# Moving 640 columns of each tile from ScalarE to VectorE in a batch-norm kernel that streams through three buffers

## The chip, the cores and the metric

The kernel runs on 1 core of one Trainium2 chip. The metric is the device time of one execution in microseconds (us), as the median of several runs. Experiments of one batch ran on the same chip as new runs of the kernel before, and each is compared with those.

## The reference

```python
# x: (32, 256, 128, 128) float32; the four parameters: 256 channels each
return gamma * (x - mean) / np.sqrt(var + eps) + beta
```

Per channel this is one multiplication and one addition, `x * scale + shift`. The kernel must read 537 MB and write 537 MB; there is next to no arithmetic per byte.

## The kernel before

The input is seen as 64 tiles of 128 partitions x 16384 columns (8 MB each; 64 KB in a row). The program keeps three tiles in on-chip memory; tile `i` uses buffer `i % 3`. Three streams run side by side: SyncE issues loads, VectorE and ScalarE compute in place, ScalarE issues stores. The parts that matter:

```python
NBUF = 3
STEP = 2560       # VectorE's first piece of a tile
VCOLS = 14336     # VectorE takes columns 0..VCOLS, ScalarE the rest
VLAST = 9216      # the same for the last tile
...
for i in range(1, NT):                                  # SyncE: the loads
    if turn:
        nc.sync.wait_ge(stored[s], 16 * turn)           # buffer free: store i-3 has landed
    inst = nc.sync.dma_start(out=bufs[s][:], in_=xr[i]).then_inc(loaded[s], 16)
    if turn:
        inst._wait_ge(vdone, 2 * (i - 1) + 1)           # tile i-1 landed, its first piece done
...
for i in range(1, NT):                                  # VectorE
    vector_part(i, 0, STEP)._wait_ge(*landed(i))
    vector_part(i, STEP, VLAST if i == last else VCOLS)
for i in range(last):                                   # ScalarE
    nc.scalar.wait_ge(vdone, 2 * (i + 1))               # VectorE is done with tile i
    inst = scalar_part(i, VCOLS)
    if i:
        inst._wait_ge(stored[(i - 1) % NBUF], ...)      # hold until store i-1 has landed
    store(i)                                            # after its own piece (adone)
```

Two waits in it are no data dependencies. A load waits for VectorE's first piece of the tile before it, and ScalarE's piece waits for the store before it. The time in which the load queue has nothing to do, from the landing of one load to the first packet of the next, is called the load gap below; the same on the other queue is the store gap. ScalarE's piece lies in the store gap, VectorE's first piece in the load gap.

## Time and profile before

| | kernel before |
|---|---|
| median of the first 3 runs | 2484.97 us (2483.55 to 2486.38) |
| VectorE busy, ScalarE busy | 508.8 us, 139.8 us |
| mean DMA rate over the span | 432 GB/s |
| ScalarE's piece; VectorE's first piece | 2.09 us; 1.61 us |
| from tile to tile (mean of 50) | 38.69 us |

Two more: from the list of DMA issues on the page, a store's median time from issue to landing,

```profile
out_dram<-t ACTq DMA_DIRECT2D x64, 36.5
```

and, from SyncE's own waits (line, what it waited for, us in total, times, longest), what holds back a load:

```profile
SPq L101 <- DMA out_dram<-t: 1398.1, 61, 68.8
SPq L102 <- DVE t L130: 985.0, 61, 16.2
```

The waits come in program order, first for the freed buffer, then for VectorE's first piece of the tile before. The second still takes some 16 us each time, so the buffer is free long before the load goes, and the loads pace themselves.

### The profile page before, as it was taken

The page shows a single profiled execution, that of the slowest core. Times are in us where ns is not written, and L with a number is a line of the kernel's source. Part 1 is how long each engine was busy: PE and PEld are TensorE (multiplying, and loading weights), DVE is VectorE, ACT ScalarE, POOL GpSimd, SP SyncE. Part 2 cuts the span into 40 slices and gives each one's busy share as a digit, 9 for nine tenths or more (in the row PEclk, how much of TensorE's full clock was granted, in tenths as well). Part 3 has the DMA queues.
Part 4 walks back from the last instruction along what each step waited for, and adds up shares of the span by engine and source line. Part 5 has one row for each costly group of instructions (what it writes and reads, how often), then busy time and mean ns, then how long its engine had stood idle before and what let it go on. Part 6 is the DMA issues. An engine that isn't in the chain of part 4 may idle for free.

```text
span 2483.3 us, 516 instructions
## 1 busy us (share of the span) xinstructions
DVE 508.8 (20%) x139; ACT 139.8 (6%) x66; POOL 0.2 (0%) x4
## 2 busy tenths in 40 slices
DVE  3122121221212212122121221212212122121220
ACT  0000000000000000000000000000000000000001
POOL 0000000000000000000000000000000000000000
DMA  9999999999999999999999999999999999999999
GB/s 415 430 439 434 428 436 436 435 433 430 432 433 438 430 432 433 435 424 437 437 428 436 438 436 429 437 435 430 436 437 436 430 437 435 429 437 435 433 433 408
DMA packets 18708, 1073.85 MB, mean 432 GB/s; under 512 B 2128, under 2 KB 2192, under 8 KB 2192
## 3 DMA queue, kind: packets, MB, share of 16 engines
q1 hardware_dynamic: 9488, 536.94, 50.1%
q10 hardware_dynamic: 9216, 536.88, 49.9%
q14 instruction: 4, 0.03, 0.0%
HBM read 536.94 MB, written 536.87 MB: 432 GB/s over the span
## 4 chain that ended last, share of the span: by engine, by line
DMA 93%; DVE 4%; another core or an unknown queue 1%; ACT 0%; issue 0%; SPq 0%; DVEq 0%
DMA t<-in_x_dram 93%; DVE t L130 4%; ACT t L141 0%; SPq L91 0%; DVE rows L89 0%; SPq L95 0%; DVE eps_t L107 0%; DVEq L198 0%; SPq L70 0%
## 5 line engine op out<-in xcount | busy, mean ns | idle before, releaser
L130 DVE TENSOR_SCALAR t<-t,scale_t,shift_t 128x11776 f32<-128x11776 f32 (+2 forms) x128 | 505.3, 3989 | 1930.4 <-DMA t<-in_x_dram 1930.2
L141 ACT ACTIVATE t<-t,shift_t,scale_t 128x2048 f32<-128x2048 f32 x64 | 138.2, 2159 | 2299.3 <-DMA out_dram<-t 2276.6
L108 DVE STREAM_TRANSPOSE turned<-rows 32x1024 f32<-32x1024 f32 x1 | 1.2, 1233 | 12.5 <-DMA rows<-in_running_mean_dram 12.5
L115 ACT ACT_TABLE_LOAD x1 | 1.3, 1283 | 0.9 <-SPq L70 0.9
L89 DVE MEMSET rows<- 32x1024 f32 x1 | 0.9, 912 | 1.2 <-SPq L70 1.2
L115 ACT ACTIVATE std_t<-par,eps_t 128x2 f32<-128x2 f32 x1 | 0.3, 296 | 14.7 <-DVE par L113 14.7
L113 DVE COPY par<-turned 32x8 f32<-32x8 f32 x4 | 0.6, 161 | 0.1
L122 DVE RECIPROCAL rstd_t<-std_t 128x2 f32<-128x2 f32 x1 | 0.2, 166 | 0.4 <-ACT std_t L115 0.4
L125 DVE TENSOR_TENSOR shift_t<-par,ms_t 128x2 f32<-128x2 f32 x1 | 0.2, 161 | 0.0
L124 DVE TENSOR_TENSOR ms_t<-par,scale_t 128x2 f32<-128x2 f32 x1 | 0.2, 161 | 0.0
L123 DVE TENSOR_TENSOR scale_t<-par,rstd_t 128x2 f32<-128x2 f32 x1 | 0.2, 160 | 0.0
L187 POOL MEMSET const-bfloat16-1.0<- 128x1 bf16 x1 | 0.1, 101 | 0.0
L187 POOL MEMSET const-uint8-127<- 128x1 uint8 x1 | 0.1, 101 | 0.0
L187 POOL MEMSET const-float32-0.0<- 128x1 f32 x1 | 0.1, 98 | 0.2 <-issue 0.2
L187 POOL MEMSET const-float32-1.0<- 128x1 f32 x1 | 0.1, 98 | 0.0
L107 DVE MEMSET eps_t<- 128x1 f32 x1 | 0.1, 59 | 0.1
## 6 DMA issues: line engine op xcount, KB each, us to landing
t<-in_x_dram SPq DMA_DIRECT2D x2, 4096.0 KB, 16.5
out_dram<-t ACTq DMA_DIRECT2D x64, 36.5
t<-in_x_dram SPq DMA_DIRECT2D x63, 37.0
rows<-in_running_var_dram SPq DMA_DIRECT2D x1, 16.0 KB, 11.3
rows<-in_gamma_dram SPq DMA_DIRECT2D x1, 16.0 KB, 11.1
rows<-in_beta_dram SPq DMA_DIRECT2D x1, 16.0 KB, 10.9
rows<-in_running_mean_dram SPq DMA_DIRECT2D x1, 16.0 KB, 11.3
```

The lines of the kernel that those rows point to most:

```text
L89: zeroed = step(nc.vector.memset(rows[:], 0.0))
L107: step(nc.vector.memset(eps_t[:], eps))
L108: step(nc.vector.transpose(out=turned[:], in_=rows[:]), fetched, 16 * NPAR)
L113: placed = step(nc.vector.tensor_copy(out=flat[q * B : (q + 1) * B], in_=blocks[:, :, q, 0]))
L115: nc.scalar.activation(out=std_t[:], in_=var_t, func=mybir.ActivationFunctionType.Sqrt, bias=eps_t[:], scale=1.0,)._wait_ge(vec, placed).t ...
L122: step(nc.vector.reciprocal(out=rstd_t[:], in_=std_t[:]), act, 1)
L123: step(nc.vector.tensor_mul(out=scale_t[:], in0=gamma_t, in1=rstd_t[:]))
L124: step(nc.vector.tensor_mul(out=ms_t[:], in0=mean_t, in1=scale_t[:]))
L125: ready = step(nc.vector.tensor_sub(out=shift_t[:], in0=beta_t, in1=ms_t[:]))
L130: return nc.vector.tensor_scalar(out=t[:, first:end], in0=t[:, first:end], scalar1=scale_t[:, cb : cb + 1], scalar2=shift_t[:, cb : cb + 1 ...
L141: return nc.scalar.activation(out=t[:, first:], in_=t[:, first:], func=mybir.ActivationFunctionType.Identity, bias=shift_t[:, cb : cb + 1] ...
L187: nc = _bacc.Bacc("TRN2", target_bir_lowering=False, num_devices=1)
```

## The change

The intent is to shorten what stands between the landing of one store and the issue of the next: ScalarE gets 1408 columns in place of 2048, VectorE the 640 others, for which it has time.

```diff
-VCOLS = 14336
+VCOLS = 14976
```

## The prediction

> **What bounds the kernel now.** I read first the page's totals (busy engines, the 40 slices, the DMA queues), because they say which resource is full:
>
> ```profile
> DVE 508.8 (20%) x139; ACT 139.8 (6%) x66; POOL 0.2 (0%) x4
> ...
> DMA  9999999999999999999999999999999999999999
> ...
> DMA packets 18708, 1073.85 MB, mean 432 GB/s; under 512 B 2128, under 2 KB 2192, under 8 KB 2192
> ...
> q1 hardware_dynamic: 9488, 536.94, 50.1%
> q10 hardware_dynamic: 9216, 536.88, 49.9%
> ```
>
> VectorE works a fifth of the time and ScalarE a sixteenth. The 16 DMA engines are busy in every slice, and the loads (q1) and stores (q10) take half of the engines' time each: 50.1% + 49.9% = 100%.
>
> Second I read the groups of instructions with shapes kept apart, and the waits, because there ScalarE seems to be in the way:
>
> ```profile
> L130 DVE TENSOR_SCALAR t<-t,scale_t,shift_t 128x11776 f32<-128x11776 f32 x62 | 397.3, 6408 | 0.0
> L141 ACT ACTIVATE t<-t,shift_t,scale_t 128x2048 f32<-128x2048 f32 x63 | 131.8, 2093 | 2286.9 <-DMA out_dram<-t 2276.6 <-DVE t L130 10.2
> L130 DVE TENSOR_SCALAR t<-t,scale_t,shift_t 128x2560 f32<-128x2560 f32 x63 | 101.6, 1613 | 1929.0 <-DMA t<-in_x_dram 1929.0
> L141 ACT ACTIVATE t<-t,shift_t,scale_t 128x7168 f32<-128x7168 f32 x1 | 6.4, 6360 | 12.5 <-DMA t<-in_x_dram 12.5
> ```
>
> By the program, ScalarE holds back its piece of a tile until the store of the tile before has landed, computes 2.09 us, and only then issues the next store. So in every tile the store queue has nothing to do for the landing, those 2.09 us and the start of the next DMA. That looks like a serial 2.09 us per tile, and it is what the change cuts.
>
> Third I asked whether the engines really idle in that gap. The timeline of two tiles gives the times, and the table of stretches the DMA load; its columns after the stretch are its length, the busy time and count of VectorE, ScalarE and GpSimd, the clock, the DMA share and GB/s:
>
> ```profile
> 1041.67 2.09 ACT L141 ACTIVATE t<-t,shift_t,scale_t 128x2048 f32<-128x2048 f32 x1 [36.53 <-DMA out_dram<-t]
> 1043.80 0.34 ACTq L154 DMA_DIRECT2D out_dram<-t  x1
> 1056.18 7.94 DVE L130 TENSOR_SCALAR t<-t,scale_t,shift_t 128x2560 f32<-128x2560 f32 x2 [30.69 <-DMA t<-in_x_dram]
> 1080.80 2.09 ACT L141 ACTIVATE t<-t,shift_t,scale_t 128x2048 f32<-128x2048 f32 x1 [37.03 <-DMA out_dram<-t]
> ```
>
> ```profile
> 100.00:500.00 400.00, 79.36 (x20) 21.64 (x11) 0.00 (x0) 1.00 1.00 434
> ...
> 1042.00:1047.00 5.00, 0.00 (x0) 1.76 (x1) 0.00 (x0) 1.00 1.03 446
> 1056.20:1061.40 5.20, 5.20 (x2) 0.00 (x0) 0.00 (x0) 1.00 1.02 441
> ```
>
> The second row is a store gap: ScalarE computes, and the DMA share is still 1.03 (rounding of packets that cross the edge). The DMA view of the same 5 us says who fills it: the load queue alone, with 102.9% of the engines' time and 34 packets, none of the store queue. The third row is the mirror image, a load gap (a landed tile waits for VectorE's first 1.61 us before the next load is issued), and there the store queue alone fills the engines. In the packet records of the trace a 64 KB packet takes 2.418 us on its engine, in either gap as in between, and from 1.95 us after the start to 2481.7 us no moment has fewer than 16 packets in flight. **The kernel is bound by the bytes through the 16 DMA engines.** The chain of waits names one line above all, and it goes through loads and VectorE's first piece, with ScalarE at 0%:
>
> ```profile
> DMA t<-in_x_dram 93%; DVE t L130 4%; ACT t L141 0%; SPq L91 0%; DVE rows L89 0%; SPq L95 0%; DVE eps_t L107 0%; DVEq L198 0%; SPq L70 0%
> ```
>
> **What the Trainium skill says.** "DMA: Bandwidth & Descriptors", section "Queues, rings and completion order" (its paragraph on arbitration): each engine goes round-robin between the queues that have work, a packet at a time. The trace agrees: away from the gaps, packets of q1 and q10 alternate on an engine, and in a gap the other queue's packets follow each other without a pause. The same page, "Where 436 GB/s comes from", gives a ceiling of 435 GB/s for the 16 engines; the trace has 434 in the steady stretches, so nothing is left there. "ScalarE: Activation LUTs", section "What ACT_TABLE_LOAD costs", gives 0.833 ns per element of a row whatever the function; the two ACTIVATE rows above give (6360 - 2093) / (7168 - 2048) = 0.833, the same.
>
> **The change, part by part.** No instruction is added or removed; the order of instructions on each engine is the same, only the shapes differ. 63 of the 64 tiles change; the last keeps its split at 9216.
> - ScalarE: 640 columns fewer in each of 63 tiles, 640 x 0.833 = 533 ns. An ACTIVATE goes from 2.09 to 1.56 us, and 63 x 0.533 = 33.6 us of work leave ScalarE (139.8 to about 106).
> - VectorE: 640 columns more. The slope from its two rows is (6408 - 1613) / (11776 - 2560) = 0.520 ns per column, so +333 ns a tile: the large piece goes from 6.41 to 6.74 us, 63 x 0.333 = 21.0 us more in all (508.8 to about 530).
> - VectorE's first piece (2560 columns, 1.61 us), which lets the next load go, does not change, so the load gap does not.
> - On the path to a store: ScalarE waits for VectorE too. The tile that lands at 1056.18 is done by VectorE at 1064.12, and ScalarE takes it at 1080.80, since it must wait for the store ahead: 16.7 us of slack, of which the extra 0.33 us takes 2%. The store is therefore issued 0.53 us sooner after the store ahead has landed: its gap (landing at about 1041.67 to the issue at 1043.80) shrinks from 2.13 to 1.60 us.
> - What that saves of the span: the engines were full of load packets in that gap. Of the 0.53 us nothing is saved; the store takes turns a little sooner and the load, which had them, gets them a little later. Steady state: 0 us.
> - Head: the first store comes after VectorE's second piece of tile 0 (+0.33 us) and ScalarE's (-0.53 us), 0.2 us sooner; loads fill the engines then. Tail: the last tile's split is unchanged and it waits for bytes. Together I put 0 to 0.3 us on both.
>
> The sum is 0 to -0.3 us. As a check from above: all 1073.85 MB at the steady 434 GB/s take 2474 us, so even an ideal head and tail would give only 11 us (0.4%).
>
> **Rivals.**
> 1. The store chain sets the time. Then the whole 33.6 us would come off: 2451 us, 1.4% less. For it speaks ScalarE's wait of 2276.6 us for stores, which looks like a serial loop of 38.6 us a tile. Against it: the DMA share of 1.03 in the gap. A store lands in 36.5 us because it shares the engines with loads; it has no speed of its own to which a gap is added. Even this rival stays within 2%.
> 2. VectorE becomes the bound, or the store starts to wait for it: +21 us at most, 2506 us (0.8% slower). Against it: 20% busy, 16.7 us of slack per tile.
> 3. The phases of the two streams shift. Now a store lands 14.5 us before a load does, and each gap is covered by the other queue. A shorter store gap (unchanged load gap) favours the stores in the round-robin; they could run ahead, until a store waits for its own tile and both gaps fall together, and then engines could idle. How far: the store's first packet reaches the engines 3.1 to 3.4 us after its issue; 0.53 us is 22% of a 2.418 us packet, so per tile on about a fifth of the engines the store would get in a turn sooner, and these are engines whose load part ends early anyhow (the packet records show six that end their load some 3 to 4 us ahead of the last), so neither landing need move. Should the stores gain on the loads all the same, they have the 16.7 us of slack to use up first, and then VectorE's wait stops them while the next load has already been issued. I expect at most a few us here, 1% for more than 50 us.
> 4. Contention or bad luck of a run: single tiles now and then take 1 us longer (37.7 in place of 36.5 us of waiting), and the three times before spread from 2483.55 to 2486.38.
>
> **Range and chances.** From 2484.97 us I take 0.2 for the head and leave the rest: **2484.8 us**. The range is the spread of runs of the kernel before widened by about 2 us on each side for a shifted phase: 2481.5 to 2488.5. Faster by over 2% would need 2435 us, less than the bytes take at 434 GB/s, so 0.5%; slower by over 2% (2535 us) needs 0.8 us of idle engines in every tile: 1%; within 2%: 98.5%.
>
> **What would show it.** In the profile after: ScalarE's row at about 1.56 us with about 106 us in all, VectorE's large piece at 6.74 us, the DMA share still 1.00 and 433 to 434 GB/s in the steady stretches, a time from tile to tile still near 38.65 us, and the waits of ScalarE for stores grown by what its work lost (2276.6 + 33.6 = about 2310 us). Step by step wrong would be: a period of 38.1 us (rival 1), ScalarE waiting for VectorE in steady state (2 or the end of 3), a DMA share under 0.99 or a store that lands much nearer to the load (3). The prediction fails if the engines turn out to have idle time between the two queues that the records hide, or if a changed phase opens such time.

## The result, and the profile after

| | before | after |
|---|---|---|
| median of 6 runs each | 2482.99 us (2482.05 to 2486.38) | 2483.53 us (2482.64 to 2487.21) |
| ratio | | 1.0003, 95% interval 0.9990 to 1.0016 |
| ScalarE busy, VectorE busy | 139.8, 508.8 us | 106.2, 529.9 us |
| from tile to tile (mean of 50 in the profiled run) | 38.69 us | 38.73 us |

A ratio is the mean time of one kernel's runs over that of the other's of the same rounds, so it is not quite the ratio of the medians. Nothing came of the change: same, within 0.16%. (The profiled run of the changed kernel was the slowest of its six, 2487.21 us.)

The page's totals after:

```profile
DVE 529.9 (21%) x139; ACT 106.2 (4%) x66; POOL 0.2 (0%) x4
...
DMA  9999999999999999999999999999999999999999
...
q1 hardware_dynamic: 9488, 536.94, 50.1%
q10 hardware_dynamic: 9216, 536.88, 49.8%
```

The groups with shapes kept apart (busy us and mean ns of one; after the second bar the idle time before them and its causes):

```profile
L130 DVE TENSOR_SCALAR t<-t,scale_t,shift_t 128x12416 f32<-128x12416 f32 x62 | 418.0, 6742 | 0.0
...
L141 ACT ACTIVATE t<-t,shift_t,scale_t 128x1408 f32<-128x1408 f32 x63 | 98.2, 1559 | 2322.6 <-DMA out_dram<-t 2311.7 <-DVE t L130 10.9
```

The two pieces changed exactly as their slopes say, and ScalarE's wait for stores grew from 2276.6 to 2311.7 us: the 35 us look like the 33.6 us of work that went away. The list of DMA issues says the same per tile, since a store now lands later after its issue:

```profile
out_dram<-t ACTq DMA_DIRECT2D x64, 37.1
```

The timeline shows the distances inside a tile:

```profile
1041.60 1.56 ACT L141 ACTIVATE t<-t,shift_t,scale_t 128x1408 f32<-128x1408 f32 x1 [37.03 <-DMA out_dram<-t]
1043.18 0.34 ACTq L154 DMA_DIRECT2D out_dram<-t  x1
1056.14 8.27 DVE L130 TENSOR_SCALAR t<-t,scale_t,shift_t 128x2560 f32<-128x2560 f32 x2 [30.37 <-DMA t<-in_x_dram]
1080.27 1.56 ACT L141 ACTIVATE t<-t,shift_t,scale_t 128x1408 f32<-128x1408 f32 x1 [37.12 <-DMA out_dram<-t]
```

From the landing of a store (ScalarE's start) to its issue it is now 1.58 us, before 2.13 us. But the load lands 14.54 us after ScalarE's start, where before it was 14.51, and the next ScalarE start follows at 38.67 us. The store was offered 0.5 us earlier and finished no earlier. The table of stretches shows the steady state and a store gap (columns: length, busy time and count of VectorE, ScalarE and GpSimd, clock, DMA share, GB/s):

```profile
100.00:500.00 400.00, 82.70 (x20) 16.49 (x11) 0.00 (x0) 1.00 1.00 435
1042.00:1046.50 4.50, 0.00 (x0) 1.15 (x1) 0.00 (x0) 1.00 1.08 466
```

The engines are as full as they were. A short stretch like the second gives a share a little off 1, as packets that start in it are counted whole.

### The profile page after: what moved, and what is told of

It reads as the page before. It is cut to its first block, busy times and chain, and to the rows that moved or that the text cites. A ratio compares the mean times of both kernels' runs of the same rounds, so it can differ in the third digit from the quotient of the medians.

```text
span 2485.4 us, 516 instructions
## 1 busy us (share of the span) xinstructions
DVE 529.9 (21%) x139; ACT 106.2 (4%) x66; POOL 0.2 (0%) x4
## 4 chain that ended last, share of the span: by engine, by line
DMA 92%; DVE 5%; another core or an unknown queue 2%; ACT 0%; issue 0%; SPq 0%; DVEq 0%
DMA t<-in_x_dram 92%; DVE t L130 4%; ACT t L141 0%; SPq L91 0%; DVE rows L89 0%; DVE eps_t L107 0%; DVEq L198 0%; SPq L70 0%
## 5 line engine op out<-in xcount | busy, mean ns | idle before, releaser
L130 DVE TENSOR_SCALAR t<-t,scale_t,shift_t 128x12416 f32<-128x12416 f32 (+2 forms) x128 | 526.4, 4154 | 1911.9 <-DMA t<-in_x_dram 1911.8
L141 ACT ACTIVATE t<-t,shift_t,scale_t 128x1408 f32<-128x1408 f32 x64 | 104.6, 1634 | 2335.6 <-DMA out_dram<-t 2311.7
```

Of the source, the lines that this page charges most:

```text
L130: return nc.vector.tensor_scalar(out=t[:, first:end], in0=t[:, first:end], scalar1=scale_t[:, cb : cb + 1], scalar2=shift_t[:, cb : cb + 1 ...
L141: return nc.scalar.activation(out=t[:, first:], in_=t[:, first:], func=mybir.ActivationFunctionType.Identity, bias=shift_t[:, cb : cb + 1] ...
```

## The experiments

The theory of the prediction is that the gap on one queue costs nothing because the other queue fills the engines. Its rivals are a store chain that does set the time (with the gain lost elsewhere), and a phase between the two streams that the gap helps to set. If the gap is simply free, it is free at any size; so the first batch made much larger changes to the same waits.

To see the order of packets, the packet records of the trace were strung together. The records don't name the engine; a record was put behind the one that ended as it started, so single swaps between engines are possible. Below, L is a 64 KB packet of a load and S of a store, `S.` and `L.` are a store's and a load's closing 4-byte packet alone, a number in brackets the duration in ns where it was over 2500 (2418 otherwise), and `--1.51--` an idle engine for 1.51 us. One engine's row from the kernel before:

```
S L S L S. L L L S L S L. S S S L S L S L S L S. L
```

The store ends (`S.`), load packets run alone until the next store comes, both take turns, the load ends (`L.`), store packets run alone, and so on: eight packets of each in a tile (the closing ones not counted), 16 x 2.418 = 38.69 us, which is the measured time from tile to tile.

### Shorter still: ScalarE 128 columns (e1_scalar128)

```diff
-VCOLS = 14336
+VCOLS = 16256
```

> ScalarE computes 128 columns ahead of each store (about 0.49 us by the slope of 0.833 ns a column), VectorE the rest: three times the step of the change, in the same direction. Theory 'the DMA engines are full, so the store gap is free': 2483 us, the same as before. Rival 'the store chain sets the time': 63 x 1.60 us = 101 us less, 2383 us. Rival 'phase': the store gap is now shorter than the load gap by over a us, the stores gain on the loads until a store waits for its own tile; both gaps then fall near each other and engines idle: slower than 2535 us, and ScalarE is seen waiting for VectorE.

Measured: **2562.86 us** (2558.87 to 2569.82), ratio 1.0332, 95% interval 1.0315 to 1.0350. Taking three times as much from ScalarE's piece made the kernel 3.3% slower. Both "free at any size" and "the store chain sets the time" fall. ScalarE's waits name the mechanism that the phase rival had named:

```profile
ACT t L141 <- DMA out_dram<-t: 1233.6, 32, 43.7
ACT t L141 <- DVE t L130: 1216.4, 31, 41.0
```

Before, ScalarE waited 62 times for a store and once for VectorE; now in half of the tiles the store ahead lands before VectorE is done with the tile. The time from ScalarE's start to the next landing of a load, tile by tile from the second on, shows how it gets there (us):

```
before         14.52 14.50 14.53 14.52 14.54 14.51 14.52 ... 14.51 14.56
after          14.60 14.56 14.51 14.63 14.52 15.27 14.52 ... 14.51 14.56
e1_scalar128   16.93 21.74 26.61 31.86 29.16 31.61 28.85 ... 29.35 31.44
```

In the kernel before and in the changed one this distance stays put. In e1 the stores gain 4.8 us, two packets, on the loads in each tile, until they run into VectorE. Then the two gaps overlap. One engine's row:

```
S S. --1.51-- L(3238) L L L(3518) S L S L S L S L S L. S S S
```

The store has ended, the load that should fill the gap isn't there yet, and the engine idles for 1.5 us, the longest in this gap (most of the 16 idle 0.5 to 1.4 us). The first load packet after it takes 3.24 us in place of 2.42, and the last one before the stores come back 3.52. The table of stretches, with the same columns as above, shows that the DMA share doesn't betray this, but the rate does:

```profile
1500.00:2000.00 500.00, 107.22 (x24) 5.91 (x12) 0.00 (x0) 1.00 1.00 421
```

The sum agrees. Between 500 and 2000 us the mean load packet took 2548 ns, before 2427: 8 x 0.121 = 0.97 us a tile. Idle engines took 0.56% of the time, 0.22 us of a tile of 39.9. Together 1.19 us, over some 62 tiles 74 us; measured were 80. So most of the loss is in longer packets, not in idle engines.

### Longer: ScalarE 7680 columns (e2_scalar7680)

```diff
-VCOLS = 14336
+VCOLS = 8704
```

> ScalarE computes 7680 columns ahead of each store (about 6.8 us), VectorE 5632 fewer: the opposite direction, nine times the step. Theory 'free gap': 2483 us, since 8 load packets of 2.418 us would cover a gap of 10.4 us. Rival 'store chain': 63 x 4.69 = 296 us more, 2779 us. Rival 'phase': the store gap is twice the load gap, the loads run ahead until each waits for a freed buffer, that is for the store to land; then the engines idle from that landing to the load's first packet (about 3.7 us by the records): some 60 x 3.7 = 220 us more, about 2700 us, with the DMA share of the steady stretches near 0.91 and SyncE waiting last for stores.

Measured: **2729.20 us**, ratio 1.0990, 1.0974 to 1.1006. This direction also costs, and close to what the phase rival gave (2700), with the mark that it named: SyncE waits last for stores now,

```profile
SPq L101 <- DMA out_dram<-t: 2587.6, 61, 69.2
```

and no longer for VectorE. Loads run ahead, end some 7.2 us before the store does, and each then waits for the buffer that the store will free. From that landing on nothing is queued. In the packet records around the landing that ScalarE sees at 1527.65 us, the last store packets end, engine by engine, between 1526.21 and 1527.27 us; the load is issued at 1527.69, and its first packets start between 1528.65 and 1529.07. The engines idle about 2 us each, and over a longer stretch the share and the rate fall:

```profile
1500.00:2000.00 500.00, 60.02 (x24) 79.01 (x12) 0.00 (x0) 1.00 0.95 394
```

Idle engines take 4.9% of a period of 42.5 us (2.1 us), longer load packets (2647 ns) 8 x 0.220 = 1.76 us: 3.9 us a tile, over 62 tiles 239 us; measured were 247. The share that the expectation gave, 0.91, was off: nearly half of the loss is in longer packets, not in idle engines. So were the 3.7 us from the landing to the load's first packet: with the engines idle it is 1.0 us here.

### The load gap longer: a first piece of 8192 columns (e3_first8192)

```diff
-STEP = 2560
+STEP = 8192
```

> VectorE's first piece, on which the next load waits, is 8192 columns in place of 2560 (4.55 in place of 1.61 us); ScalarE as before. Theory 'free gap', applied to the load gap: 2483 us. Rival 'the chain of waits is a chain of durations' (load, first piece, load): 62 x 2.94 = 182 us more, 2665 us. Rival 'phase': as with a store gap that is too short, stores catch up with the loads and engines idle: over 2535 us, with ScalarE waiting for VectorE.

Measured: **2681.10 us**, ratio 1.0802, 1.0786 to 1.0818. A longer load gap is no more free than a longer store gap. By its size the run doesn't tell a serial chain (2665) from the phase; ScalarE's waits and the last run of the next batch (e6_both_long) do. A serial load chain would leave ScalarE waiting for stores; it waits for VectorE:

```profile
ACT t L141 <- DVE t L130: 2326.0, 59, 42.0
```

### No hold on the stores (e4_no_hold)

```diff
-            inst = scalar_part(i, VCOLS)
-            if i:
-                inst._wait_ge(stored[(i - 1) % NBUF], 16 * ((i - 1) // NBUF + 1))
+            scalar_part(i, VCOLS)
             store(i)
```

> ScalarE does not hold its piece back for the store ahead, so each store is issued when its tile is ready, and the store queue has no gap by ScalarE at all. Theory 'free gap': 2483 us. Rival 'store chain': the whole gap of 2.13 us and the start of the DMA fall away, at least 63 x 2.13 = 134 us less, 2349 us. Rival 'phase': with no store gap the stores always catch up with the loads and then wait for their own tile; the engines idle in part of each tile: over 2535 us.

Measured: **2553.95 us**, ratio 1.0288, 1.0269 to 1.0308. The result is correct, and in the code the wait orders no data, as the tile and the store ahead of it use different buffers. It looks like a wait that costs; taking it out costs 2.9%. ScalarE's waits are now for VectorE, 63 times, and the rate falls as in e1:

```profile
ACT t L141 <- DVE t L130: 2343.9, 63, 41.4
...
1500.00:2000.00 500.00, 95.22 (x24) 25.11 (x12) 0.00 (x0) 1.00 1.00 421
```

So the hold, with ScalarE's piece behind it, is what keeps the stores from overtaking the loads.

### Both gaps shorter, both gaps longer (e5_both_short, e6_both_long)

If what counts is the balance of the two gaps, then e1 and e3 can be mended from the other side, by a change that on its own should be neutral or bad.

```diff
 e5_both_short            e6_both_long
-STEP = 2560             -STEP = 2560
+STEP = 256              +STEP = 8192
-VCOLS = 14336           -VCOLS = 14336
+VCOLS = 16256           +VCOLS = 10816
```

> ScalarE 128 columns as in e1_scalar128 (store gap 1.60 us shorter than before), and VectorE's first piece 256 columns (load gap about 1.2 us shorter too). Theory 'what counts is the balance of the two gaps': both are shorter by nearly the same, the stores no longer catch up with the loads, and the time comes back to about 2483 us from the 2563 of e1_scalar128, with ScalarE waiting for stores. Rival 'a store gap this short is bad in itself' (the store would start before a packet boundary where it hurts): it stays near 2563 us.

> VectorE's first piece 8192 columns as in e3_first8192 (load gap 2.94 us longer), and ScalarE 5568 columns, 2.93 us more than before (store gap longer by the same). Theory 'balance': back to about 2483 us from the 2681 of e3_first8192, though both queues' gaps are now half as long again as before. Rival 'a gap longer than about 5.5 us can't be hidden': 2681 us or more, since the ScalarE piece is added to it.

Measured: e5 **2486.93 us**, ratio 1.0015 (1.0000 to 1.0030); e6 **2486.96 us**, ratio 1.0012 (0.9996 to 1.0029). Both come back. e5 has e1's ScalarE piece of 0.49 us and is 76 us faster than e1; e6 has e3's first piece of 4.55 us and on top of it a ScalarE piece of 5.03 in place of 2.09 us, and it is 194 us faster than e3. In both, ScalarE waits for stores again:

```profile
ACT t L141 <- DMA out_dram<-t: 2374.7, 62, 43.8
```

```profile
ACT t L141 <- DMA out_dram<-t: 2099.4, 62, 42.4
```

(the first is e5, the second e6). The balance is thereby shown, in both directions. `VCOLS` also moves VectorE's second piece, a rival cause of e1's loss; but both pieces together take VectorE 8.94 us a tile in e1 and in e5 alike, and e4 is slow with VectorE's pieces unchanged.

### A control with the loads away (c1_small2048, c2_small1408, then d1_tiny2048, d2_tiny1408)

Is ScalarE's time really worth something where nothing fills the gap? For this the loads were cut down from the fourth tile on, so that the results are wrong. In the c pair each later load moves 512 columns:

```diff
+            few = slice(0, 512) if i >= NBUF else slice(0, HW)
-            inst = nc.sync.dma_start(out=bufs[s][:], in_=xr[i]).then_inc(loaded[s], 16)
+            inst = nc.sync.dma_start(out=bufs[s][:, few], in_=xr[i][:, few]).then_inc(loaded[s], 16)
```

with `VCOLS` at 14336 in c1 and 14976 in c2.

> Wrong result on purpose: from the fourth tile on each load moves 512 columns of 16384, so stores run nearly alone; ScalarE 2048 columns as in the kernel before. Every theory: per tile 8 store packets of 2.418 us on each engine (19.3 us) and the store gap from landing to first packet (about 5.7 us) with nothing to fill it, 25 us a tile, about 1.6 to 1.7 ms in all. It is the partner of the next run.

> The same with 1408 columns, as in the changed kernel. Theory 'the gap is free only because loads fill it': here nothing fills it, so the 0.533 us of each tile come off the time, 60 to 63 x 0.533 = 32 to 34 us less than its partner (2%). Rival 'the change is lost on something else, such as VectorE's extra 0.33 us or ScalarE's own waits': no or a clearly smaller difference, or more time.

Measured: c1 1524.87 us, c2 **1528.88 us**: 4 us more, not 33 less. The expectation missed. The trace says why the pair is a bad control. In c1 the little loads wait for the freed buffer and fall into the store gap (in one gap all 128 packets landed within 2.7 us of their issue); in c2 VectorE's first piece releases them last, they start 1.8 us later, beside the store, and lengthen it: ScalarE waits 21.4 us a tile for it in place of 20.8. So even loads of 256 KB, moved from the gap to the side of the store, gave back what ScalarE had saved.

The d pair does it again with 2 KB for each engine (16 partitions x 512 columns):

```diff
+            few = (slice(0, 16), slice(0, 512)) if i >= NBUF else (slice(0, P), slice(0, HW))
-            inst = nc.sync.dma_start(out=bufs[s][:], in_=xr[i]).then_inc(loaded[s], 16)
+            inst = nc.sync.dma_start(out=bufs[s][few], in_=xr[i][few]).then_inc(loaded[s], 16)
```

> Wrong result on purpose, a cleaner control than c1_small2048: from the fourth tile on a load moves one 2 KB packet on each engine, so that it can't matter whether it falls into the store gap or beside the store. ScalarE 2048 columns. About 8 x 2.418 = 19.3 us of store packets and 3.6 us of gap a tile (the gap of c1_small2048), near 22.9 us a tile, about 1520 us. Partner of the next run.

> The same with 1408 columns. Theory 'ScalarE's time counts where nothing fills the gap': 60 x 0.533 = about 32 us less than its partner. Rival 'it is lost elsewhere, even with the loads away': within 10 us of its partner, as in the c pair.

Measured: d1 1522.48 us (1522.35 to 1522.67), d2 **1490.35 us** (1490.29 to 1490.40): 32.1 us less. The same edit that did nothing in the full kernel gives its whole 0.53 us a tile here. The timelines, d1 then d2:

```profile
1179.07 2.09 ACT L142 ACTIVATE t<-t,shift_t,scale_t 128x2048 f32<-128x2048 f32 x1 [20.80 <-DMA out_dram<-t]
...
1201.95 2.09 ACT L142 ACTIVATE t<-t,shift_t,scale_t 128x2048 f32<-128x2048 f32 x1 [20.79 <-DMA out_dram<-t]
```

```profile
1176.57 1.56 ACT L142 ACTIVATE t<-t,shift_t,scale_t 128x1408 f32<-128x1408 f32 x1 [20.79 <-DMA out_dram<-t]
...
1198.96 1.56 ACT L142 ACTIVATE t<-t,shift_t,scale_t 128x1408 f32<-128x1408 f32 x1 [20.83 <-DMA out_dram<-t]
```

The wait for the store stays at 20.8 us, and the shorter piece shortens the period, on average of 50 tiles from 22.93 to 22.40 us. In the full kernel the wait grew by what the piece lost. That is the difference between work on the path and work beside a full resource.

### The edges of the flat stretch (e7_scalar768, e8_scalar4096)

```diff
 e7_scalar768             e8_scalar4096
-VCOLS = 14336           -VCOLS = 14336
+VCOLS = 15616           +VCOLS = 12288
```

> ScalarE 768 columns ahead of each store, 1.07 us less than before, one more step of the change's size: the near edge of the flat stretch. Theory 'the phases lock within a fraction of a packet of 2.418 us': if the edge lies beyond, 2483 us with the load landing some 14.5 us after ScalarE's start in every tile; if it lies before, the distance grows by up to two packets a tile until ScalarE waits for VectorE, and the time is between 2500 and 2565 us. Rival 'free gap at any size': 2483 us; rival 'store chain': 2416 us.

> ScalarE 4096 columns, 1.71 us more than before: the far edge. Theory 'lock': flat at 2483 us with a steady distance, or, if the edge lies before, loads ahead of the stores until SyncE waits last for stores, with 2550 to 2730 us. Rival 'store chain': 63 x 1.71 = 108 us more, 2591 us, with a steady distance and a period of 40.4 us.

Measured: e7 **2513.08 us**, ratio 1.0108 (1.0061 to 1.0155), with runs from 2495.04 to 2517.91; e8 **2655.53 us**, ratio 1.0692 (1.0676 to 1.0708). Both are off the flat stretch: e7 by 1.1%, with an interval clear of 1. e7 lies on its edge, which may explain the wide spread of its runs (only one of them was profiled). In its profiled run the distance from ScalarE's start to the next landing, from the second tile on, holds for 13 tiles and then slips in steps of about 2.4 us, one packet:

```
14.50 15.34 14.66 14.54 14.52 14.56 14.66 14.55 14.50 14.54 14.51 14.58 14.50
16.96 19.38 19.33 21.78 24.16 24.20 24.16 26.62 31.62 29.44 30.28 ...
```

The end that the expectation gave, ScalarE waiting for VectorE, came only 4 times; 59 times it still waited for a store. e7 is slower without that wait: its load packets take 2475 ns on average between 500 and 2000 us, before 2427.

In e8 the distance falls to 4.8 us and stays there, with a period of 41.55 us: load and store land so near to each other that the gaps overlap. Between 500 and 2000 us engines idle 2.1% of the time (0.86 us a tile), and load packets take 152 ns and store packets 97 ns longer than before: 2.85 us a tile, over 62 tiles 177 us; measured were 172. My expectation that SyncE would wait last for stores was wrong: it still waits last for VectorE (6.6 us each),

```profile
SPq L101 <- DMA out_dram<-t: 2139.7, 61, 66.9
SPq L102 <- DVE t L130: 403.0, 61, 13.7
```

so this is a third state, steady and slow, between the flat stretch and e2's.

### All runs by the balance of the two gaps

The change of each gap against the kernel before is the difference of the durations in the groups of instructions (ScalarE's piece: 2.093 us before, 1.559 with 1408 columns, 1.026 with 768, 0.493 with 128, 3.799 with 4096, 5.026 with 5568, 6.79 with 7680; first piece 1.613, 0.413 with 256 columns, 4.546 with 8192).

| run | store gap | load gap | difference | time, us | ratio to before |
|---|---|---|---|---|---|
| e3_first8192 | 0 | +2.93 | -2.93 | 2681.10 | 1.0802 |
| e1_scalar128 | -1.60 | 0 | -1.60 | 2562.86 | 1.0332 |
| e7_scalar768 | -1.07 | 0 | -1.07 | 2513.08 | 1.0108 |
| after | -0.53 | 0 | -0.53 | 2483.53 | 1.0003 |
| e5_both_short | -1.60 | -1.20 | -0.40 | 2486.93 | 1.0015 |
| before | 0 | 0 | 0 | 2482.99 | 1 |
| e6_both_long | +2.93 | +2.93 | 0.00 | 2486.96 | 1.0012 |
| e8_scalar4096 | +1.71 | 0 | +1.71 | 2655.53 | 1.0692 |
| e2_scalar7680 | +4.69 | 0 | +4.69 | 2729.20 | 1.0990 |

The time follows the difference of the gaps, not either gap. In the kernel before the gaps themselves are nearly equal: from the last closing packet to the next first packet, 5.8 us for loads and 6.2 us for stores (medians). The time is flat at least from -0.53 to 0, and the change stayed inside. Its far edge lies between 0 and +1.71 us; where, no run shows.

## Why the prediction was right, point by point

- **The bound and the time.** 2484.8 us was said, 2483.53 measured, in the range. That the kernel is bound by the bytes through the 16 engines holds for both kernels: 434 to 435 GB/s in the steady stretch between 100 and 500 us. Two of its readings of the packet records were a little too smooth: fewer than 16 packets are in flight for 0.6 us in all, and of the load packets between 500 and 2000 us 127 of 4935 take over 2.5 us, up to 3.6, in place of 2.418. In the changed kernel they are 219 of 4932.
- **The costs of the parts.** ScalarE's piece was put at 1.56 us and is 1.559, VectorE's large one at 6.74 and is 6.742; their totals were put at 106 and 530 us and are 106.2 and 529.9.
- **What becomes of the 33.6 us.** The wait for stores was to grow to about 2310 us; it is 2311.7. The d pair shows that these us are real where the engines are not full (32.1 us), and that it is the loads that hide them.
- **Rival 1** (the store chain, 2451 us) is refuted by the result, and by e1, which would have had to gain 101 us and lost 80. **Rival 2** (VectorE) is refuted by ScalarE's waits: one for VectorE in the changed kernel, as before.
- **Rival 3** (the phase) was seen, but its size was wrong, and this is the weak step of a prediction that came out right. It said of the state in which the stores run into VectorE "I expect at most a few us here". e1 is in that state and costs 80 us. The two reasons given against it were of unequal worth. That the store's earlier offer of 0.53 us need not move either landing held: the distance stayed at 14.5 us. That VectorE's wait stops the stores "while the next load has already been issued" did not help. In e1 most of the store's packets end some 2 us after a load lands; the next load is issued 1.6 us after that landing (VectorE's first piece) and its first packet comes 1.0 us later still (1570.02, 1571.66 and 1572.62 us in the tile shown). Engines idle before it, and packets near the pause take longer. The prediction also named no size at which the phase is lost. It lies between 0.53 and 1.07 us, and the change was 0.53: that the change stayed inside was partly luck.
- **A mark that would not have worked.** The prediction named a DMA share under 0.99 as the sign of a shifted phase. e1 and e4 have 0.99 to 1.00 and are 3% slower; the rate, 421 in place of 434 GB/s, and the durations of load packets show it.
- **What the chain of waits says.** It names loads and VectorE's first piece, before and after:

```profile
DMA t<-in_x_dram 92%; DVE t L130 4%; ACT t L141 0%; SPq L91 0%; DVE rows L89 0%; DVE eps_t L107 0%; DVEq L198 0%; SPq L70 0%
```

It tells which events follow from which, not that a longer link makes the whole longer by as much: e6 lengthens both that first piece and ScalarE's by 2.9 us a tile, and the time stays.

What stays open: why load packets take 3 us and more after a pause and where the stores come back (only that they do is shown), and where in the 1.7 us above the kernel before the flat stretch ends.

## What to carry to other kernels

When two queues share full DMA engines, work in the gap of one queue is hidden by the other, so shortening it gains nothing; check this by asking what the engines did in the gap, not who waited how long. But the gap isn't free at any size: in this kernel the two queues' gaps had to match to within part of one packet's time (0.53 us of difference cost nothing, 1.07 us did, with packets of 2.418 us), or the streams drifted until the gaps overlapped. Waits that look superfluous may be what keeps them apart, and if one gap must change, change the other by as much.

## What the Trainium skill lacked or had wrong

- "DMA: Bandwidth & Descriptors", section "Queues, rings and completion order", has the round-robin between queues by packets, which these traces agree with. It lacks what follows for two streams of large packets: the distance between them locks in steps of a packet of 2.418 us (14.5 us before and after, 12.1 in e6, 21.75 in e5, 17.0 for a few tiles in e5: 6, 5, 9 and 7 packets), holds at no cost for a difference of the gaps from -0.53 to 0 us, is lost at -1.07 us, and at +1.71 us settles two packets apart (4.8 us) with the gaps overlapping. The time off the flat stretch grew by 1.1 to 9.9%.
- The same page, section "Issuing engines are not separate DMA queues", says that issuing from several engines only saves the sequencer's time. No run here issues both streams from one engine, so that isn't contradicted; but with two issuers the moment at which each issues decided over 3 to 10% (e1, e2, e3, e4, e8), which the section doesn't mention.
- No page that I found has the longer load packets of these states: just after an idle stretch of their engine 3.1 us (median in e1 and e2) in place of 2.418, and just before the stores come back 3.6 us (median in e2). In e1 this took 0.97 us a tile against 0.22 us of idle engines. An idle engine is not needed for it: in e8 first load packets with no idle time before them take 3.4 us (median).
- "Perfetto Trace Analysis", section "Identifying the Most-Contended Engine", calls occupancy misleading for the 16 DMA engines and advises HBM utilization, a measure of what was moved, in its place. The runs agree, and give a number: e4 has a share of 1.00 and 421 GB/s, the kernel before 1.00 and 434.
